# Values of the residue grouping with queries on partitions, in a hybrid DeltaNet and dilated-attention layer

## The chip, the cores and the metric

The kernel runs on one core of one Trainium2 chip. The metric is the time of the device for one execution, in microseconds (us); the time of a kernel is the median of its runs.

## The reference

One decoder layer on a sequence of 2048 positions with a model width of 1024. One input projection feeds two groups of heads; their outputs are concatenated, multiplied by `w_out`, gated, added to `x` and normalised. What matters here is the attention group: 8 heads of width 64, three patterns of causal attention whose results are merged by the softmax of their log-sum-exps.

```
PATTERNS = ((128, 1), (512, 4), (2048, 16))
for window, dilation in PATTERNS:
    o, lse = strided_window_attention(q, k, v, dilation, window // dilation)
    outs.append(o); lses.append(lse)
wts = jax.nn.softmax(jnp.stack(lses, axis=0), axis=0)
o_at = jnp.sum(wts[..., None] * jnp.stack(outs, axis=0), axis=0)
o_at = rmsnorm(o_at, at_norm_w) * jax.nn.silu(at_z)
mix = jnp.concatenate([o_dn, o_at], axis=-1) @ w_out
```

Each position sees, per pattern, itself and earlier positions at steps of the dilation, up to the window.

## The kernel before, in words

The kernel has three stages, one after the other. The first (projections, the chunked delta rule) isn't touched. The second is the attention, and the third what is left of the output projection.

**The attention.** The heads are worked on in 4 pairs `p`, and the sequence in 4 blocks `blk` of 512 positions. Within a block there are 8 units of work. Four belong to grouping *a* (the pattern of dilation 1): 128 queries against at most 256 neighbouring keys. Four belong to grouping *b*, the grouping by residues `r` of the position modulo 4: 128 queries of one residue against all keys of that residue so far, `(blk + 1) * 128` of them, with one mask that serves both the pattern of dilation 4 and that of dilation 16. So for each pair there are 4 units of *b* with one tile of 128 keys, 4 with two, 4 with three and 4 with four.

A unit has three steps. `scores` (L1211) multiplies queries and keys into PSUM (tile `s`), adds the mask and takes the extremum on VectorE (`sm`), and exponentiates on ScalarE (`p`, queries on partitions). `turn` (L1236) transposes `p` on TensorE, 128x128 at a time, two tiles of keys and both heads to a PSUM bank `tr` (two banks), and copies each bank to SBUF (`pts`, keys on partitions), three in four copies on VectorE and the fourth on ScalarE. `values` (L1255) multiplies by the values: for each tile of keys `k` and each head `hd` of the pair, a matmul whose stationary operand (`lhsT`) is the head's 64 columns of `v`, and whose moving operand (`rhs`) is the head's 128 columns of `pts`. The output stands with the 64 value columns on partitions: head 0 on partitions 0 to 63, head 1 on 64 to 127, of one PSUM bank `po` (a single buffer), 128 queries per unit side by side. In the fourth unit of a grouping ScalarE copies the bank to SBUF, as `oa` (L1369) or `ob` (L1384).

All data is fp32. Queries and keys are split into fp32r halves; `p`, `pts` and `v` are plain fp32, and a plain fp32 matmul of the program is two weight loads and two MATMUL instructions in the trace. A transposition is one of each.

**The merge.** `combine` (L1263) runs once per pair and block, 16 times, as a generator in the queue `aux`. It sends the statistics of grouping *a* through DRAM (`sscr`) to bring them to the order of *b*, waits some units of work, forms the two weights `ca` and `cb` per query and head, and then, for `oa` and for `ob` (L1288 to L1295): takes a bank `tr`, transposes four 128x128 pieces so that queries stand on partitions, multiplies the bank by the weight on VectorE into `cmb`, and yields. The two are added on GpSimd, normalised, transposed back and stored.

**The order of the work.** `attention` (L1389) issues for each unit: its scores; the values of the unit before the last; the transpositions of the last unit. After each of the two yields the driver (L1650) takes one step of the filler queue `side` in every second turn (L1651), which is up to four matmuls of 512 columns of the output projection (`mix_dn` L1552 and `mix_at` L1574; tiles `ip<-w_..,m_..`), and one step of each generator in `aux`. Waits inside generators (`hop`, L213) are counted in TensorE time that the kernel itself adds up for each matmul and transposition (`Counted`, L141). What is left of `mix_at` when the attention has ended runs by itself, through the banks `s`.

Of the kernel before, what the change touches and what calls it, by code (L numbers as in the profile page):

```python
# [21 lines left out]
P = 128  # L22
# [90 lines left out]
def kernel(ctx: ExitStack, tc: tile.TileContext, x, c_t, pos, w_mod, b_mod_t, b_gate,  # L113
# [45 lines left out]
    T, TE, VO, AO = Counted(nc.tensor), Counted(Early(nc.tensor)), InOrder(nc.vector), InOrder(nc.scalar)  # L159
    dma = nc.sync.dma_start  # L160

    def flat(t):
        return t.rearrange("p a b -> p (a b)")
# [6 lines left out]
    def bank(tag, bufs=2):  # L170
        return psum.tile([P, 512], F32, name=tag, tag=tag, bufs=bufs)
# [41 lines left out]
    def hop(n=HOP):  # L213

        end = spent[0] + n * TICK
        yield
        while spent[0] < end:
            yield
# [3 lines left out]
    ident, le, gt, m16, cols = (cst[:, i] for i in range(5))  # L222
# [53 lines left out]
    def rsqrt(pool, y, a, tag):  # L276

        u = pool.tile(list(y.shape), F32, name="rs_u", tag=tag + "_u")
        V.tensor_scalar(y.bitcast(I32), a.bitcast(I32), -0.5, 1597463007.0, op0=OP.mult, op1=OP.add)
        for _ in range(3):  # L280
            V.tensor_tensor(u, y, y, OP.mult)  # L281
            V.scalar_tensor_tensor(u, u, -0.5, a, op0=OP.mult, op1=OP.mult)  # L282
            V.scalar_tensor_tensor(y, u, 1.5, y, op0=OP.add, op1=OP.mult)
# [971 lines left out]
    def values(pts, v, po, q):  # L1255
        for k, p_ in enumerate(pts):
            for hd in range(2):
                T.matmul(po[64 * hd:64 * hd + 64, q * P:q * P + P], lhsT=v(k)[:, 64 * hd:64 * hd + 64],
                         rhs=p_[:, hd], start=k == 0, stop=k == len(pts) - 1)

    combined = [0] * 4

    def combine(pool, p, blk, oa, ob, sta, sb):  # L1263

        gz = pool.tile([P, 4, P], F32, name="agz", bufs=1)
        dma(gz, zscr[p, :, :, blk * P:(blk + 1) * P])
        sa = pool.tile([P, 4, 4], F32, name="stc", bufs=2)
        d = sscr[p, blk]
        dma(d, sta)
        for b in range(4):  # L1270
            dma(sa[32 * b:32 * b + 32], bass.AP(tensor=d.tensor, offset=d.offset + 4 * b,
                                                ap=[[16, 32], [512, 4], [1, 4]]))
        yield from hop(LAG)
        w = pool.tile([P, 4, 4, 2], F32, name="cw_", bufs=2)
        mn, ca, cb, l = (w[:, i] for i in range(4))
        V.tensor_tensor(mn, sa[:, :, 0:2], sb[:, :, 0:2], OP.min)
        V.tensor_tensor(ca, mn, sa[:, :, 0:2], OP.subtract)
        V.tensor_tensor(cb, mn, sb[:, :, 0:2], OP.subtract)
        A.activation(w[:, 1:3], w[:, 1:3], AF.Exp)
        V.tensor_tensor(l, ca, sa[:, :, 2:4], OP.mult)  # L1280
        V.tensor_tensor(mn, cb, sb[:, :, 2:4], OP.mult)
        V.tensor_tensor(l, l, mn, OP.add)
        V.scalar_tensor_tensor(l, l, EPS, l, op0=OP.mult, op1=OP.mult)
        yield
        B4 = [P, 4, 2, 64]
        v4 = "p (t h d) -> p t h d"
        parts = []
        for o_, c_ in ((oa, ca), (ob, cb)):  # L1288
            ps = bank("tr")
            for k in range(4):  # L1290
                T.transpose(ps[:, k * P:k * P + P], o_[:, k * P:k * P + P], ident)
            c = pool.tile(B4, F32, name="cmb", bufs=CMB)
            V.tensor_tensor(c, ps.rearrange(v4, t=4, h=2), c_[:, :, :, None].to_broadcast(B4), OP.mult)
            parts.append(c)
            yield  # L1295
        o, sq = parts
        G.tensor_tensor(o, o, sq, OP.add)
        A.activation(sq, o, AF.Square)
        ssq = pool.tile([P, 4, 2], F32, name="a_ssq", bufs=2)
        V.tensor_reduce(ssq, sq, axis=AX.X, op=OP.add)  # L1300
        V.scalar_tensor_tensor(ssq, ssq, 1.0 / 64, l, op0=OP.mult, op1=OP.add)
        rs = pool.tile([P, 4, 2], F32, name="a_rs", bufs=2)
        rsqrt(pool, rs, ssq, "a")
        G.tensor_tensor(o, o, rs[:, :, :, None].to_broadcast(B4), OP.mult)
        yield from hop(LAG2)
        ps = bank("tr")
        of = o.rearrange("p t h d -> p (t h d)")
        for k in range(4):
            T.transpose(ps[:, k * P:k * P + P], of[:, k * P:k * P + P], ident)
        oc = pool.tile([P, J], F32, name="a_oc", bufs=1)  # L1310
        V.scalar_tensor_tensor(oc, ps, nwz[:, 1:2], flat(gz), op0=OP.mult, op1=OP.mult)
        dma(oscr[1][p, :, :, blk * P:(blk + 1) * P], oc.rearrange("p (r i) -> p r i", r=4))
        combined[blk] += 1
# [3 lines left out]
    def pair_blocks(pool, p):  # L1317

        ks = ahead["k"]
        va, vb = [], []  # L1320
        for blk in range(4):
            (qs, qa), v = ahead["q"], ahead["v"]
            if blk == 1:
                if p < 3:
                    ahead["k"], ahead["load"] = load_k(p + 1)
                else:
                    ya, yb = ahead["y"] = [hp.tile([P, 4, D], F32, name=f"y_{nm}", tag=f"h_{nm}", bufs=2)
                                           for nm in ("hi", "lo")]
                    dma(ya[:, 0], gscr)
                    aux.append(load_w(raws, 4, ya[:, 0], lambda j: yb[:, j // 2, j % 2 * J:j % 2 * J + J], WLAG))  # L1330
            if blk and p < 3:
                ahead["load"](blk - 1, blk)
            elif p and blk == 0:
                ahead["load"](3, 4)
            if blk < 3 or p < 3:
                at = (p, blk + 1) if blk < 3 else (p + 1, 0)
                ahead["q"] = load_q(akp, *at)
                ahead["v"] = load_v(pool, *at)
            va.append(v[0])
            vb.append(v[1])  # L1340
            sta = pool.tile([P, 4, 4], F32, name="sta", bufs=3)
            stb = pool.tile([P, 4, 4], F32, name="stb", bufs=3)
            V.memset(sta, 0.0)
            V.memset(stb, 0.0)
            oa = pool.tile([P, J], F32, name="oa", bufs=2)
            ob = pool.tile([P, J], F32, name="ob", bufs=2)
            box = {}
            for i in range(4):
                b = 4 * blk + i
                n = 256 if b else 128  # L1350

                def part(j, b0, m):
                    return lambda kk: kk[:, j].rearrange("p (r b i) -> p b r i", r=4, b=4)[:, b0:b0 + m]

                if b and not i:
                    rhs = [(slice(0, P), part(blk - 1, 3, 1)), (slice(P, n), part(blk, 0, 1))]
                else:
                    rhs = [(slice(0, n), part(blk, max(i - 1, 0), n // P))]

                def s1(i=i, n=n, rhs=rhs, qa=qa, sta=sta):  # L1360
                    return scores(pool, ks, qa, n, mask_a[:, 256 - n:], sta, i, lambda q: q[:, i], rhs)

                def s3(pts, i=i, b=b, n=n, box=box, oa=oa):
                    if i == 0:
                        box["a"] = bank("po", PO)
                    b0 = b - (n // P - 1)
                    values(pts, lambda k: va[(b0 + k) // 4][:, (b0 + k) % 4], box["a"], i)
                    if i == 3:
                        A.copy(oa.rearrange("p (r b i) -> p r b i", r=4, b=4),  # L1369
                               box["a"].rearrange("p (b r i) -> p r b i", b=4, r=4))  # L1370

                yield s1, lambda pp, n=n: turn(pool, pp, n), s3
            n = (blk + 1) * P
            for r in range(4):
                def s1(r=r, n=n, qs=qs, stb=stb):
                    return scores(pool, ks, qs, n, mask_b[:, J - n:], stb, r, lambda q: q[:, r],
                                  [(slice(0, n), lambda kk: kk[:, 0:n // P, r * P:r * P + P])])

                def s3(pts, r=r, blk=blk, box=box, oa=oa, ob=ob, sta=sta, stb=stb):
                    if r == 0:  # L1380
                        box["b"] = bank("po", PO)
                    values(pts, lambda k: vb[k][:, r], box["b"], r)
                    if r == 3:
                        A.copy(ob, box["b"])  # L1384
                        aux.append(combine(pool, p, blk, oa, ob, sta, stb))

                yield s1, lambda pp, n=n: turn(pool, pp, n), s3
# [362 lines left out]
```

## Time and profile before

| | |
|---|---|
| median of 3 runs | 1560.82 us (1558.38 to 1561.52) |
| the profiled execution | 1564.69 us, its span 1562.9 us |
| TensorE matmuls busy | 1433.8 us (92%) |
| VectorE, ScalarE, GpSimd busy | 1066.2, 656.0, 466.1 us |
| mean granted TensorE clock | 0.975 of 2.4 GHz |

The times stand in microseconds from the start of the span. PE is TensorE's matmul side and PEld its weight loads, which overlap the matmuls; DVE is VectorE, ACT ScalarE, POOL GpSimd, SP the engine that issues the DMAs. A matmul's recorded time contains the latency through the array, so matmuls that follow each other overlap in the record: the spacing of their starts, not the mean time of one, is what one costs. In a timeline, a row of x16 instructions has the start of the first and the time to the end of the last.

### The profile page before, as it was taken

The page shows a single profiled execution, that of the slowest core. Times are in us where ns is not written, and L with a number is a line of the kernel's source. Part 1 is how long each engine was busy: PE and PEld are TensorE (multiplying, and loading weights), DVE is VectorE, ACT ScalarE, POOL GpSimd, SP SyncE. Part 2 cuts the span into 40 slices and gives each one's busy share as a digit, 9 for nine tenths or more (in the row PEclk, how much of TensorE's full clock was granted, in tenths as well). Part 3 has the DMA queues.
Part 4 walks back from the last instruction along what each step waited for, and adds up shares of the span by engine and source line. Part 5 has one row for each costly group of instructions (what it writes and reads, how often), then busy time and mean ns, then how long its engine had stood idle before and what let it go on. Part 6 is the DMA issues. An engine that isn't in the chain of part 4 may idle for free.

```text
span 1562.9 us, 28358 instructions
## 1 busy us (share of the span) xinstructions
PE 1433.8 (92%) x9848; PEld 1156.7 (74%) x9848; DVE 1066.2 (68%) x3305; ACT 656.0 (42%) x1864; POOL 466.1 (30%) x573
## 2 busy tenths in 40 slices
PE   3898999989879999998999999998899998999997
PEld 2687787767767787876777779886677776777776
DVE  6868745684786367587687766434476776889766
ACT  4435234335433753433243343222455554576444
POOL 2424253333452432041231320223121211142243
PEclk9999999999999999999999999999999999999999
DMA  8845562546573642454434515438877637363364
GB/s 245 277 135 192 162 206 81 176 133 212 178 225 97 226 132 87 155 177 129 152 99 129 159 39 154 148 106 259 248 224 212 205 108 229 89 197 104 105 226 162
DMA packets 256336, 257.08 MB, mean 164 GB/s; under 512 B 44993, under 2 KB 196673, under 8 KB 255681
## 3 DMA queue, kind: packets, MB, share of 16 engines
q1 hardware_dynamic: 253744, 246.88, 51.1%
q10 hardware_dynamic: 2448, 8.39, 1.4%
q8 instruction: 78, 1.28, 0.3%
q14 instruction: 66, 0.53, 0.1%
HBM read 164.31 MB, written 90.90 MB: 163 GB/s over the span
## 4 chain that ended last, share of the span: by engine, by line
PE 36%; DVE 10%; DMA 4%; ACT 2%; issue 2%; POOL 1%; SPq 1%; DVEq 0%; ACTq 0%; POOLq 0%
PE ip L149 16%; PE s L149 8%; PE tr L154 5%; PE po L149 4%; PE g L149 2%; PE sc L149 2%; DVE cv_y L693 1%; DMA sscr<-sta 1%; DMA wg<-in_w_mod_dram 1%; DVE tmp_inv L807 1%; DVE rs_u L282 1%; DVE pts L1251 1%; DMA y_lo<-in_w_out_dram 1%; DVE sm L1226 1%; DVE rs_u L281 0%
## 5 line engine op out<-in xcount | busy, mean ns | idle before, releaser
L149 PE MATMUL ip<-h_hi,w_hi 128*128 128x512 f32 x864 | 352.8, 410 | 6.0 <-ACT cv_r L688 4.7
L149 PE MATMUL ip<-h_hi,w_lo 128*128 128x512 f32 x864 | 352.6, 410 | 0.0
L149 PE MATMUL ip<-h_lo,w_hi 128*128 128x512 f32 x864 | 352.5, 410 | 0.0
L149 PEld LDWEIGHTS ip<-h_hi,w_hi 128*128 128x128 f32 x864 | 165.9, 192 | 39.3 <-ACT cv_r L688 5.6
L149 PEld LDWEIGHTS ip<-h_lo,w_hi 128*128 128x128 f32 x864 | 165.3, 191 | 32.2 <-issue 0.5
L149 PEld LDWEIGHTS ip<-h_hi,w_lo 128*128 128x128 f32 x864 | 165.1, 191 | 32.2 <-issue 0.8
L693 DVE SCALAR_TENSOR_TENSOR cv_y<-cv_r,cw,cv_y 128x512 f32<-128x512 f32 x144 | 116.0, 805 | 32.9 <-ACT cv_y L690 23.0
L581 POOL TENSOR_TENSOR w_lo<-w_raw,w_hi 128x512 fp32r<-128x512 f32 x72 | 97.0, 1357 | 112.4 <-ACT w_hi L580 84.7
L1226 DVE CUSTOM_DVE_ANT_0 sm<-s,mask 128x256 f32<-128x256 f32 (+3 forms) x256 | 107.9, 447 | 21.4 <-PE s L149 10.7
L154 PE MATMUL tr<-cst,p 128*128 128x128 f32 x568 | 95.3, 289 | 4.2 <-ACT p L1229 2.7
L1251 DVE COPY pts<-tr 128x512 f32<-128x512 f32 (+1 forms) x120 | 73.1, 616 | 30.7 <-PE tr L154 29.2
L1229 ACT ACTIVATE p<-sm,stb 128x128 f32<-128x128 f32 (+3 forms) x128 | 70.9, 555 | 52.4 <-DVE stb L1226 39.9
L1229 ACT ACTIVATE p<-sm,sta 128x256 f32<-128x256 f32 (+1 forms) x128 | 63.2, 495 | 68.7 <-DVE sta L1226 61.9
L154 PEld LDWEIGHTS tr<-cst,p 128*128 128x128 f32 x568 | 62.1, 142 | 25.4 <-issue 14.6
L695 ACT ACTIVATE cv_t<-cv_y 128x512 f32<-128x512 f32 x48 | 30.3, 631 | 117.6 <-DVE cv_y L693 114.1
L149 PE MATMUL ip<-w_hi,h_hi 128*128 128x264 f32 (+1 forms) x256 | 75.4, 295 | 2.0 <-DVE rp L1033 1.3
L149 PE MATMUL ip<-w_hi,h_lo 128*128 128x264 f32 (+1 forms) x256 | 75.0, 293 | 0.0
L149 PE MATMUL ip<-w_lo,h_hi 128*128 128x264 f32 (+1 forms) x256 | 74.9, 293 | 0.0
L807 DVE TENSOR_TENSOR tmp_inv<-xt_inv,blk 128x8 f32<-128x8 f32 (+14 forms) x240 | 65.6, 273 | 6.4
L580 ACT CAST w_hi<-w_raw 128x512 fp32r<-128x512 f32 x72 | 43.6, 617 | 49.4 <-DMA w_raw<-in_w_in_dram 40.9
L138 ACT ACTIVATE sqo<-o 128x128 f32<-128x128 f32 x64 | 19.8, 309 | 103.0 <-DVE o L138 97.3
L1041 POOL TENSOR_TENSOR rp<-rx,tab 128x512 f32<-128x512 f32 x32 | 41.5, 1312 | 57.5 <-ACT rx L1031 48.5
(470 smaller groups left out, 3372.9 us busy)
## 6 DMA issues: line engine op xcount, KB each, us to landing
w_raw<-in_w_in_dram SPq DMA_DIRECT2D x72, 256.0 KB, 3.9
ws<-w_hi SPq DMA_DIRECT2D x15, 1024.0 KB, 5.5
ws<-w_lo SPq DMA_DIRECT2D x15, 1024.0 KB, 7.4
w_hi<-ws SPq DMA_DIRECT2D x15, 1024.0 KB, 6.0
w_lo<-ws SPq DMA_DIRECT2D x15, 1024.0 KB, 7.5
xt<-in_x_dram SPq DMA_DIRECT2D x24, 512.0 KB, 5.2
wm<-in_w_mod_dram SPq DMA_DIRECT2D x32, 256.0 KB, 5.4
tab<-ctab SPq DMA_DIRECT2D x32, 256.0 KB, 3.3
```

What stands on the lines that cost most here:

```text
L138: return f(*a, **k)
L149: i = self.engine.matmul(ps, lhsT=lhsT, rhs=rhs, **k)
L154: i = self.engine.transpose(*a)
L580: A.copy(hi[:, s, 0:256], raw)
L581: G.tensor_tensor(lo[:, s, 0:256], raw, hi[:, s, 0:256], OP.subtract)
L693: V.scalar_tensor_tensor(y, r[:, n:n + J], cw[:, ti, n:n + 1], y, op0=OP.mult, op1=OP.add)
L695: A.activation(t, y, AF.Tanh)
L807: V.tensor_tensor(tmp[:, :, 0:i + 1], xt[:, :, 0:i + 1], b3[:, i:i + 1, 0:i + 1].to_broadcast([P, 4, i + 1]), OP.mult)
L1041: G.tensor_tensor(p2, xs[1 - ct], tab[1], OP.mult)
L1226: V.tensor_tensor_reduce(out=sm, in0=pp[hd], in1=masks, scale=-0.125, scalar=BIG, op0=OP.add, op1=OP.min, accum_out=st[:, slot, hd:hd + 1])
L1229: A.activation(pt, sm, AF.Exp, scale=-1.0, bias=st[:, slot, hd:hd + 1], accum_out=st[:, slot, 2 + hd:3 + hd])
L1251: V.tensor_copy(pts[:, 0:kn], pt[:, 0:kn])
```

## The change

A second function for the values is added and used in grouping *b* alone: the transposed probabilities become the stationary operand (128 columns) and the head's 64 columns of `v` the moving one, so that the output stands with queries on partitions and the 64 value columns of each head side by side. `combine` then takes `ob` as it is; `oa` is transposed as before. `oa` keeps the old function.

```
+    def values_q(pts, v, po, q):
+        for hd in range(2):
+            c = slice(q * P + 64 * hd, q * P + 64 * hd + 64)
+            for k, p_ in enumerate(pts):
+                T.matmul(po[:, c], lhsT=p_[:, hd], rhs=v(k)[:, 64 * hd:64 * hd + 64],
+                         start=k == 0, stop=k == len(pts) - 1)
@@ combine
         for o_, c_ in ((oa, ca), (ob, cb)):
-            ps = bank("tr")
-            for k in range(4):
-                T.transpose(ps[:, k * P:k * P + P], o_[:, k * P:k * P + P], ident)
+            ps = o_
+            if o_ is oa:
+                ps = bank("tr")
+                for k in range(4):
+                    T.transpose(ps[:, k * P:k * P + P], o_[:, k * P:k * P + P], ident)
             c = pool.tile(B4, F32, name="cmb", bufs=CMB)
             V.tensor_tensor(c, ps.rearrange(v4, t=4, h=2), c_[:, :, :, None].to_broadcast(B4), OP.mult)
@@ pair_blocks, grouping b
-                    values(pts, lambda k: vb[k][:, r], box["b"], r)
+                    values_q(pts, lambda k: vb[k][:, r], box["b"], r)
```

## Rows read from the trace of the kernel before

**Rows 1.** Engines' busy time over the whole span, from the page

```profile
PE 1433.8 (92%) x9848; PEld 1156.7 (74%) x9848; DVE 1066.2 (68%) x3305; ACT 656.0 (42%) x1864; POOL 466.1 (30%) x573
```

**Rows 2.** Busy time in two stretches: the attention, and what follows it

```profile
core 0: us, PE busy (x) PEld busy (x) DVE busy (x) ACT busy (x) POOL busy (x), PEclk, DMA share, GB/s
1114.00:1465.50 351.50, 334.76 (x2712) 264.18 (x2711) 268.14 (x1002) 199.29 (x620) 85.37 (x84) 0.99 0.58 168
1465.50:1563.00 97.50, 84.89 (x374) 69.19 (x371) 64.90 (x170) 40.27 (x91) 37.79 (x30) 0.94 0.52 181
```

**Rows 3.** Groups of instructions: count, busy us, mean ns, idle us before them

```profile
L149 PE MATMUL po<-pts,vb 128*64 128x128 f32 x640 | 50.6, 285 | 4.6 <-ACT pts L1249 2.5 <-ACT oa L1369 1.1 <-DVE pts L1251 0.9
...
L154 PE MATMUL tr<-cst,ob 128*128 128x128 f32 x64 | 10.3, 285 | 4.1 <-DVE cmb L1293 4.0
...
L149 PE MATMUL g<-g,ones 128*128 128x32 f32 x4 | 0.8, 276 | 0.0
```

**Rows 4.** Timeline of PE around a values group with four key tiles

```profile
1454.75 0.39 PE L149 MATMUL ip<-w_lo,m_hi 128*128 128x512 f32 x1
1455.07 1.09 PE L149 MATMUL po<-pts,vb 128*64 128x128 f32 x16
1456.09 1.09 PE L154 MATMUL tr<-cst,p 128*128 128x128 f32 x8
```

**Rows 5.** Timeline of PE around one with a single key tile

```profile
1219.96 0.44 PE L149 MATMUL po<-pts,vb 128*64 128x128 f32 x4
1220.33 0.44 PE L154 MATMUL tr<-cst,p 128*128 128x128 f32 x2
```

**Rows 6.** Timeline of PE, a values group cut after its first, second and third pair

```profile
1301.42 0.33 PE L149 MATMUL po<-pts,va 128*64 128x128 f32 x2
...
1301.42 0.44 PE L149 MATMUL po<-pts,va 128*64 128x128 f32 x4
...
1301.42 0.55 PE L149 MATMUL po<-pts,va 128*64 128x128 f32 x6
```

**Rows 7.** Timeline of PE: filler, transpositions of `ob`, the next values group

```profile
1209.70 0.39 PE L149 MATMUL ip<-w_lo,m_hi 128*128 128x512 f32 x1
1209.93 0.60 PE L154 MATMUL tr<-cst,ob 128*128 128x128 f32 x4
1210.46 0.66 PE L149 MATMUL po<-pts,va 128*64 128x128 f32 x8
1211.05 0.44 PE L154 MATMUL tr<-cst,p 128*128 128x128 f32 x2
```

**Rows 8.** Timeline of PE: plain fp32, 128 stationary and 32 moving columns

```profile
593.49 0.60 PE L149 MATMUL g<-g,cst 128*128 128x32 f32 x4 [0.57 <-DVE sc L751]
593.92 0.39 PE L149 MATMUL g<-g,ones 128*128 128x32 f32 x2
```

**Rows 9.** Waits of the weight loads in the attention: total, times, longest

```profile
PEld tr L154 <- issue: 17.9, 93, 1.4
PEld po L149 <- issue: 14.3, 51, 0.5
PEld tr L154 <- ACT p L1229: 5.9, 21, 1.6
PEld tr L154 <- DVE cmb L1293: 4.5, 2, 4.3
PEld po L149 <- DVE sta L1226: 4.1, 12, 0.4
```

**Rows 10.** Timeline of the longest stop of PE in the attention

```profile
1305.01 0.66 PE L154 MATMUL tr<-cst,p 128*128 128x128 f32 x4
...
1308.96 0.69 DVE L1293 TENSOR_TENSOR cmb<-tr,cw__14528 128x512 f32<-128x512 f32 x1 [5.24 <-DMA sscr<-sta]
...
1309.71 1.12 PE L154 MATMUL tr<-cst,ob 128*128 128x128 f32 x4 [4.04 <-DVE cmb L1293]
```

**Rows 11.** VectorE's products of two tensors, one operand in PSUM, or both in SBUF

```profile
L1045 DVE TENSOR_TENSOR rpc<-rp,rp 128x512 f32<-128x512 f32 x32 | 38.0, 1206 | 11.2 <-POOL rp L1041 11.2
...
L1157 DVE TENSOR_TENSOR mf_x<-ip,mf_x 128x512 f32<-128x512 f32 x8 | 5.5, 690 | 18.7 <-PE ip L149 10.0 <-DMA mf_x<-in_x_dram 6.6 <-issue 2.0
```

## The prediction

> **What bounds the kernel now.** I read the busy times of the whole page first [rows 1]: TensorE's matmuls are busy 92% of the span, VectorE 68%. A share of the whole span says nothing of one stage, so I then asked for the busy times of the two stretches that the change can touch [rows 2]: in the attention (351.5 us) PE is busy 95% and VectorE 76%, and in the 97.5 us behind it PE 87%. Overlapping records make PE look fuller than it is, so the third view is a timeline of PE around one values group [rows 4]: filler, values, transpositions follow each other, and no row names an engine that PE waited for. The waits of the weight loads [rows 9] show the same: the largest by far are "issue" (17.9 and 14.3 us), in which nothing else is late. Waits for other engines sum to some ten microseconds beside them (the softmax 5.9, one bank 4.5; the 12 equal waits of 0.3 to 0.4 us put down to `sta` look like the "issue" ones under another name). So the attention is bound by TensorE's own sequence, and microseconds added to or taken from it there should show nearly one for one. Behind it comes more TensorE work, which only moves.
>
> **How a values group costs what it does.** Grouping *b* has 16 units each with one, two, three and four key tiles (4 pairs x 4 residues). A key tile is two heads with two MATMULs each, so the groups have 4, 8, 12 and 16 instructions: 16 x 40 = 640, the count of [rows 3].
>
> Now: cut after one, two and three pairs, a group reaches 0.33, 0.44 and 0.55 us [rows 6]. The second instruction of a pair adds nothing, each pair adds 0.11. The two heads write different halves of the partitions, and their matmuls run side by side. An instruction thus costs 0.055 us.
>
> At the edges it costs more. From the last filler to the group pass 0.32 us [rows 4], from a filler to transpositions 0.23 [rows 7]: 0.09 more. Four transpositions behind a values group take 0.66 us [rows 10], four behind a filler 0.60 [rows 7]: 0.06 more. The group itself, from its start to the next, takes 1.02 us with 16 instructions [rows 4] and 0.37 with four [rows 5]; 12 instructions between them cost 0.65, and the rest is a fixed part of 0.15. So there is a toll of 0.15 + 0.09 + 0.06 = 0.30 us per group, paid on the way into and out of the half-width form. The whole comes to 0.09 + 0.37 + 0.06 = 0.52 for four instructions, 1.17 for 16 and, on the line between, 0.74 and 0.95. Sum 3.38, times 16: 54.1 us.
>
> The Trainium skill, "TensorEngine Tiling (Array Packing)", section When to Use Tiling, speaks against the change: for a moving width of up to 64 it says to swap the operands so that the narrow one is stationary and two column tiles work at once, and that is the form which is given up here. The trace agrees that this form works (pairs, 0.11 us each); what the page's advice leaves out of its factor of two is the toll, 64 x 0.30 = 19 us here.
>
> **The change, part by part.**
>
> *Values.* The instruction count stays at 640. All 128 columns of the array are now stationary, so nothing runs side by side, and the moving width is 64. The trace has no fp32 matmul of just this shape; the nearest has 128 stationary and 32 moving columns [rows 8]. Four of these need 0.43 us from their start to the next row's (0.108 each); the next two take 0.39, less the 0.276 of one [rows 3], 0.114. I take 0.111: with a quarter of the moving columns of a transposition it is no cheaper, so the weight load sets the pace, and 64 columns still lie under it. The floor would be 0.055 (half of the 0.11 that a pair of 128 columns needs), if the moving columns set the pace; that is the first rival. Going in, the first load lies under the filler or transposition before it, and the last matmul is out after its 64 columns, 0.055 instead of 0.111. There is no toll. So N instructions cost 0.111 N - 0.055: 0.39, 0.83, 1.28, 1.72, sum 4.22, times 16: 67.5 us. Against 54.1 that is **+13.4 us**: -0.13, +0.09, +0.33 and +0.55 per unit with one, two, three and four key tiles. If the first load isn't hidden, 64 x 0.11 = 7.0 more.
>
> *Transpositions of `ob`.* 64 go [rows 3]. Four of them push the next values group 0.53 us back [rows 7], of which 0.09 is that group's toll: 0.44 x 16 = **-7.0 us**, all of it in PE's sequence. What follows is the unit's next step, whose inputs are there; nothing new is late.
>
> *VectorE's product.* It read a PSUM bank and now reads `ob` in SBUF. With one operand in PSUM a product of two tensors takes 0.69 us, with both in SBUF up to 1.21 [rows 11]; so 16 x 0.52 = 8.3 us of VectorE's time at most, and a small gain isn't excluded. VectorE has 83 us free in the attention [rows 2], and the product is awaited by GpSimd alone: nothing. Without that cover, in the densest stretches, it would be a part of the 8.3.
>
> *Waits.* `ob` no longer takes a bank `tr`. The weight load now waits for `pts` and the matmul for `v`, before it was the other way round; both are a unit old by then, and behind them on PE the same transpositions wait. `hop` counts the same for the new matmuls and 0.43 us less per merge for the lost transpositions; the merges come a little earlier, which nothing waits for.
>
> Sum: 13.4 - 7.0 = **+6.4 us**. The rows are of one execution of 1564.69 us, 0.25% above the median of the runs; 1571.1 for that one, and 1560.8 + 6.4 = 1567.2 us for the median.
>
> **The rivals.**
>
> *A: the moving columns set the pace.* 640 x 0.055 = 35.2 us instead of 54.1, with the 7.0: -26 us, **1535 us**. It decides if PE loads the next weights faster than 0.055 us. The matmuls with 32 moving columns [rows 8] speak against it, as they would then be under 0.03 apart; for it speaks only that those are few, of another stage. The Trainium skill, "TensorE: Matmul & The Clock Gate", section Back-to-back issue gap, gives moving columns over the clock as the gap of a matmul by itself, which is this rival; its section LDWEIGHTS gives columns over 1.2 GHz, 107 ns for 128, whatever moves, which is the forecast. The trace's 0.108 to 0.114 sides with the second.
>
> *B: waits give it back.* The longest stop of PE [rows 10] ends in the transpositions of `ob`: VectorE waited 5.24 us for a store of statistics, the two banks `tr` were full, and PE stood 4.0 us. Without these transpositions scores and filler could have gone on. The transpositions behind the stop took 1.12 us instead of 0.60 [rows 7, 10], so PE was at its lower clock (1.2 instead of 2.4 GHz); a few such microseconds cost one or two more. If all of the 4.3 us and of that go, 6.0 are back: +0.4, **1561 us**. Against it: the store is just as late, and PE stops at the next transposition of `p`, which needs a bank as well.
>
> *C: the costs at their upper ends.* First loads not hidden (+7.0), and the units with one key tile, where PE does wait at times, give back nothing of their 16 x 0.13 = 2.1: 6.4 + 9.1 = +15.5, **1576 us**. Against it: weight loads overlap the matmuls before them elsewhere in the trace.
>
> **How the numbers follow.** The forecast, with its own range of 1563 to 1571, gets 0.58; A 0.08, B 0.20, C 0.14. Two measured times of this kernel can be told apart from about 0.2%, 3.1 us. Slower than 1563.9: nearly all of the forecast (0.54) and C, 0.68. Within: B's middle and the low end of the forecast, 0.20. Faster: A and the outer part of B, 0.12. The range leaves out A and the upper part of C: 1559 to 1574.
>
> **What would show it.** In the trace after: `po<-pts,vb` stays at 640, its starts some 0.11 us apart, one by one and not in pairs; a group with 16 instructions takes 1.7 us to the next row and one with four 0.4 to 0.45; transpositions behind it take 0.60 for four; "issue" waits of the weight loads fall to about half, those around *a* stay; `tr<-cst,ob` is gone; the attention is some 6 us longer, and what follows it as long as before. Starts 0.055 apart would be A. If the starts are 0.11 apart and the time doesn't rise, look at the stops of PE for B.

## The result, and the profile after

The changed kernel took 1579.51 us (median of 4 runs, 1575.51 to 1582.89) against 1561.17 us of the kernel before on the same chip (1558.38 to 1563.65): a ratio of 1.0104 [1.0085, 1.0122], slower by 18.3 us. Measured again with more runs it was 1.0062 [1.0041, 1.0084], slower by 10.6 us. Forecast were +6.4 us and a range up to 1574: the direction was right, the size was not. The profiled execution took 1579.59 us, its span 1577.8.

First the busy times of the whole page, which answer to [rows 1].

```profile
PE 1454.1 (92%) x9784; PEld 1196.9 (76%) x9784; DVE 1069.2 (68%) x3305; ACT 656.4 (42%) x1864; POOL 465.7 (30%) x573
```

64 instructions fewer on PE, 20 us more of its time. Where do they stand? Next the two stretches of [rows 2]: the attention, and what follows it.

```profile
core 0: us, PE busy (x) PEld busy (x) DVE busy (x) ACT busy (x) POOL busy (x), PEclk, DMA share, GB/s
1111.00:1482.00 371.00, 356.06 (x2678) 305.53 (x2679) 275.38 (x1027) 204.63 (x641) 84.63 (x84) 0.97 0.56 164
1482.00:1577.80 95.80, 83.20 (x372) 67.91 (x371) 64.61 (x170) 40.38 (x91) 38.15 (x30) 0.98 0.53 184
```

The attention took 371 us; before it was 351.5 in this cut. From here on I take its length from the first transposition of `p` to the last values group: 356.5 and 354.9 us in two executions of the kernel before, 370.6 and 368.4 in two of the changed one, on average +13.8. What follows took 95.8 us, against 97.5.

Now the new values groups. First the cuts of a group after one, two and three instructions, as in [rows 6], then the group in its surroundings, as in [rows 4].

```profile
1470.00 0.22 PE L149 MATMUL po<-vb,pts 128*128 128x64 f32 x1
...
1470.00 0.33 PE L149 MATMUL po<-vb,pts 128*128 128x64 f32 x2
...
1470.00 0.44 PE L149 MATMUL po<-vb,pts 128*128 128x64 f32 x3
```

```profile
1469.77 0.39 PE L149 MATMUL ip<-w_lo,m_hi 128*128 128x512 f32 x1
1470.00 1.89 PE L149 MATMUL po<-vb,pts 128*128 128x64 f32 x16
1471.73 1.04 PE L154 MATMUL tr<-cst,p 128*128 128x128 f32 x8
...
1474.44 1.89 PE L149 MATMUL po<-vb,pts 128*128 128x64 f32 x16
```

Each instruction adds 0.11 us by itself where a pair did. From filler to group pass 0.23 us (0.32 before), the group takes 1.73 to the next start (1.02 before), and eight transpositions behind it 1.04 (1.09 before): no toll. The groups with 4, 8 and 12 instructions took 0.40, 0.84 and 1.29 (medians of those outside the stretches at the lower clock).

The waits of the weight loads in the attention answer to [rows 9]. "Issue" has fallen from 17.9 and 14.3 us to somewhat less than half; the forecast said about half. The wait for VectorE's copies of `pts` has grown: the last line below is that of the kernel before.

```profile
PEld tr L154 <- issue: 7.9, 43, 0.4
PEld po L149 <- issue: 6.2, 25, 0.4
PEld po L149 <- DVE pts L1251: 6.2, 11, 2.8
PEld tr L154 <- ACT p L1229: 5.6, 18, 0.9
```

```profile
PEld po L149 <- DVE pts L1251: 2.1, 7, 0.5
```

The longest of these waits is a stop of PE, and it answers to [rows 10]. The timeline shows PE and VectorE there.

```profile
1246.59 0.69 DVE L1579 TENSOR_TENSOR m_x<-ip,m_x 128x512 f32<-128x512 f32 x1
...
1248.16 0.60 PE L154 MATMUL tr<-cst,p 128*128 128x128 f32 x4
...
1249.54 0.82 DVE L1284 TENSOR_TENSOR cw__13776<-stc,stb 128x8 f32<-128x8 f32 x1 [2.25 <-DMA stc<-sscr]
...
1250.56 0.68 DVE L1251 COPY pts<-tr 128x512 f32<-128x512 f32 x1
...
1251.30 1.16 PE L149 MATMUL po<-vb,pts 128*128 128x64 f32 x8 [2.54 <-DVE pts L1251]
```

The merge's first product of statistics (L1284) waits 2.25 us on VectorE for the DMA that brings them back from DRAM. VectorE works in its order, so a copy of transposed probabilities stands behind it, and PE stands 2.5 us for that copy. In the kernel before the longest stop lay at another merge and ended in the transpositions of `ob`. The row behind the stop has 1.16 us for eight instructions, where 1.00 is usual: within it, at 1252.2, PE's granted clock falls to 1.2 GHz, and it stays there for a while, as the next section shows.

### The profile page after: what moved, and what is told of

Its sections match the earlier page's. It is cut to its first block, busy times and chain, and to the rows that moved or that the text cites. A ratio compares the mean times of both kernels' runs of the same rounds, so it can differ in the third digit from the quotient of the medians.

```text
span 1577.8 us, 28218 instructions
## 1 busy us (share of the span) xinstructions
PE 1454.1 (92%) x9784; PEld 1196.9 (76%) x9784; DVE 1069.2 (68%) x3305; ACT 656.4 (42%) x1864; POOL 465.7 (30%) x573
## 5 line engine op out<-in xcount | busy, mean ns | idle before, releaser
L149 PEld LDWEIGHTS po<-vb,pts 128*128 128x128 f32 x640 | 81.6, 196 | 13.7 <-ACT pts L1249 3.9
L149 PE MATMUL po<-vb,pts 128*128 128x64 f32 x640 | 84.1, 276 | 7.3 <-DVE pts L1251 2.9
L154 PEld LDWEIGHTS tr<-cst,p 128*128 128x128 f32 x568 | 66.9, 150 | 16.0 <-issue 6.8
```

The lines of the kernel that those rows point to most:

```text
L149: i = self.engine.matmul(ps, lhsT=lhsT, rhs=rhs, **k)
L154: i = self.engine.transpose(*a)
```

## Experiments

All ratios are to the kernel before, measured beside each kernel on the same chip; not all kernels were measured on one chip, so those whose comparisons differ are set side by side by their ratios. Two theories run through the expectations. **ORDER**: the program's text gives dependences and priorities; the framework's scheduler makes the order of each engine from them, and with the transpositions gone it makes another one, in which the merge's work stands ahead of its data. **BANK**: the transpositions held the merge back until a bank `tr` was free, and that pacing was of use. The expectation of a size is what the prediction gave.

**The baseline and the change once more.** No edit.

> The kernel before once more, for a second trace of it. Two theories of why the change cost 18 us and not the 6.4 forecast. SEQUENCE: TensorE's own sequence in the attention grew by more than was worked out (the first pair of traces says some 10 us), and the rest, about 3 us before the attention and 3 in it, is more time at the lower clock, which comes by chance: then the stage before the attention, whose instructions are the same, varies by some 3 us between executions of any of these kernels, and the clock of this one may come out anywhere from 0.970 to 0.976. CLOCK: the changed kernel is held at the lower clock for longer because of what it does: then this one stays near 0.975 and the changed one near 0.970 every time. Time: 1561 either way.

1564.00 us, ratio 0.9990 [0.9972, 1.0009]. The mean granted clock of its profiled execution was 0.971 where it had been 0.975: the mean over the whole span changes by as much between two executions of one kernel.

> The changed kernel once more, for a second trace of it. Both theories: 1579, 1.0% above before. SEQUENCE: in the trace the attention is 10 us longer at the full clock, and the time at the lower clock differs from that of the first trace (24 us in the attention) by as much as it differs between the two traces of before. CLOCK: again 20 us or more at the lower clock in the attention, against 10 to 13 of before, and a mean clock of 0.970.

1575.80 us, 1.0062 [1.0041, 1.0084]. That the kernel before keeps to itself and the change loses about 0.6% is settled. The interval doesn't meet that of the first comparison (1.0085 to 1.0122); why isn't known. In the attention itself the time at the lower clock was 13.3 and 13.7 us in the two executions of the kernel before, and 23.9 and 20.0 us in those of the changed one.

**The values alone**: the change, with `ob` transposed nonetheless (which leaves its values in the wrong place).

```
-            if o_ is oa:
+            if True:
                 ps = bank("tr")
```

> The changed kernel with the transpositions of ob put back (they turn data the wrong way; the output is not the reference's). It isolates what their loss is worth. Forecast's term: 7.0 us, so 1586 against 1579 of the changed kernel. If they were mostly covered, 0 to 3 us (1579 to 1582): then the term of -7.0 was the one that failed.

1577.07 us, 1.0084 [1.0062, 1.0106]: +11.9 us by the medians, +13 by the ratio. The term of +13.4 holds. But the changed kernel, which has 64 transpositions fewer, is only 1.3 us faster than this by the medians (3.4 by the ratios, and the two intervals overlap), not 7.0. The traces show no gain in the attention at all: 370.6 and 368.4 us, against 367.8 with the transpositions kept. Time at the lower clock there is 23.9 and 20.0 us against 15.8, and PE's waits for VectorE's copies of `pts` are 6.2 us in the first of these against 1.5.

**Twice the moving columns**: 128 instead of 64 in `values_q` (both heads' values to the same 128 columns of the output).

```
-            c = slice(q * P + 64 * hd, q * P + 64 * hd + 64)
+            c = slice(q * P, q * P + P)
-                T.matmul(po[:, c], lhsT=p_[:, hd], rhs=v(k)[:, 64 * hd:64 * hd + 64],
+                T.matmul(po[:, c], lhsT=p_[:, hd], rhs=v(k),
```

> The changed kernel with all 128 columns of v as moving operand in each values matmul of grouping b, instead of the head's 64 (both heads write the same columns; the output is not the reference's). If the weight load sets the pace, starts stay 0.109 to 0.112 us apart and only the last of a group costs more: 64 x 0.055 = +3.5 us at most, 1579 to 1583. If the moving columns set it, starts were near 0.055 and become 0.11: +35 us. CLOCK: with twice the columns streamed the clock goes back to 0.975 and some 5 us come back: 1574 to 1578. SEQUENCE: the clock is as in the changed kernel within chance.

1578.18 us, 1.0091 [1.0068, 1.0114]: 2.4 us more than the change, not tens. Within a group the starts stand 0.112 us apart in both kernels (median), and the mean time of one instruction is nearly the same, 280 and 276 ns.

```profile
L149 PE MATMUL po<-vb,pts 128*128 128x128 f32 x640 | 85.9, 280 | 11.6 <-DVE pts L1251 6.7 <-DVE a_rs L279 2.5 <-issue 1.2
```

```profile
L149 PE MATMUL po<-vb,pts 128*128 128x64 f32 x640 | 84.1, 276 | 7.3 <-DVE pts L1251 2.9 <-ACT pts L1249 2.7 <-ACT oa L1379 1.1
```

So the moving columns don't set the pace, and rival A has no ground. What the instructions with 32, 64 and 128 moving columns share is the loading of 128 stationary ones. The trace has 13.7 us at the lower clock in the attention, 6 to 10 less than the change, and yet its attention is longer (372.7 us): the lower clock alone doesn't explain the loss.

**The loss of the transpositions alone**: the kernel before, with `ob` taken as it is (the product then has values in the wrong place).

```
-            ps = bank("tr")
-            for k in range(4):
-                T.transpose(...)
+            ps = o_
+            if o_ is oa:
+                ps = bank("tr")
+                for k in range(4):
+                    T.transpose(...)
```

> The kernel before without the transpositions of ob (its values are as before, so the product of combine reads ob the wrong way round; the output is not the reference's). The mirror of ob_kept. Forecast's term: -7.0 us against before. PARTLY COVERED (ob_kept cost 1.3 us in time, and some 4 in its trace at the full clock): -1 to -4 us.

1568.56 us, 1.0028 [1.0004, 1.0052]: the kernel with less work is *slower* by 4 us, where the sum has -7.0. The interval only just leaves out 0, but it leaves out -7.0 by far. This is the step that failed. PE's order is another one: of the 2676 matmul instructions that the trace has in the attention, at least 196 stand out of the order of the kernel before (compared by tile and shape), though only 16 groups of four transpositions were taken out. The two executions of the kernel before don't differ in a single place. PE's waits for VectorE's copies of `pts` rose from 2.1 us to 13.8, the longest 3.9:

```profile
PEld po L149 <- DVE pts L1251: 13.8, 15, 3.9
```

That longest one is a stop at the same merge as the changed kernel's:

```profile
1241.93 0.60 PE L154 MATMUL tr<-cst,p 128*128 128x128 f32 x4
...
1243.70 1.11 DVE L1276 TENSOR_TENSOR cw__13776<-stc,stb 128x8 f32<-128x8 f32 x1 [3.31 <-DMA stc<-sscr]
...
1246.22 0.66 PE L149 MATMUL po<-pts,vb 128*64 128x128 f32 x8 [3.69 <-DVE pts L1251]
```

Behind such stops stand stretches at the lower clock. Three views follow, of the kernel before, of the changed one and of this one: windows laid on the stretches of the attention whose granted clock (the third number from the end) is 0.50, that is 1.2 GHz.

```profile
1309.60:1313.00 3.40, 3.29 (x12) 2.76 (x12) 1.84 (x7) 0.88 (x4) 1.28 (x1) 0.51 0.55 154
1398.30:1405.10 6.80, 6.09 (x31) 5.02 (x31) 5.52 (x19) 4.66 (x14) 4.38 (x4) 0.50 0.73 245
```

```profile
1252.20:1255.60 3.40, 3.40 (x14) 2.88 (x13) 1.45 (x9) 2.07 (x8) 0.00 (x0) 0.50 0.36 108
1320.50:1330.70 10.20, 9.73 (x39) 8.99 (x40) 5.99 (x33) 3.68 (x15) 3.47 (x4) 0.50 0.83 255
1412.60:1419.40 6.80, 5.81 (x28) 5.81 (x29) 5.08 (x20) 3.67 (x13) 3.81 (x4) 0.50 0.63 231
```

```profile
1247.50:1250.90 3.40, 3.40 (x17) 2.42 (x15) 2.04 (x10) 1.70 (x7) 0.00 (x0) 0.50 0.46 133
1312.30:1319.10 6.80, 5.84 (x24) 4.07 (x25) 6.05 (x31) 3.56 (x14) 2.77 (x3) 0.50 0.78 244
1401.10:1411.30 10.20, 8.42 (x43) 6.83 (x43) 8.72 (x32) 6.43 (x22) 5.44 (x6) 0.50 0.47 155
```

10 us of them before, 20 after, 20 with the transpositions merely gone (a stretch of up to 3.4 us at the very start of the attention, in all three, is left out here and counted in the totals elsewhere). The first of each begins at the end of the longest stop or within 1.5 us of it; the others begin in or up to 1.8 us behind stops of 1.0 to 1.9 us. Not every such stop has one: 1.50 us at 1214.8 in the kernel before, and 1.42 at 1393.6 in this one, have none. A microsecond at half the clock loses up to half of itself, so 10 us more of them are some 5 us.

**The change in the first block only**, where groups have four instructions and are cheaper in the new form.

```
+                    (values_q if blk == 0 else values)(pts, ..., box["b"], r)
+            if o_ is oa or not (blk == 0):
```

> The new form of the values, and ob taken as it is, only in the first block of each pair, where a unit has one key tile; the other blocks as before. By the forecast's law for a group (0.111 N - 0.055 us against a toll of 0.30 and 0.055 N): 16 x -0.13 = -2.1 us for the values, and 4 of the 16 merges without transpositions, -1.0 (partly covered) to -1.8: -3 to -4 us against before. If short groups gain nothing because PE waits beside them: 0 to -1.

1563.01 us, 0.9997 [0.9976, 1.0018]: no change by the medians, where 3 to 4 us were expected; the interval reaches down to -3.7 us. It points the same way as the last one: what is taken out of PE's work doesn't come back as time.

**Fewer tolls**: the kernel before, with the values of two units issued one behind the other, PE in program order in the attention.

```
-VD = 1
+VD = 2
-                    f, pts = w2.popleft()
-                    f(pts)
+                    while w2:
+                        f, pts = w2.popleft()
+                        f(pts)
+            ordered[0] = 1      (ahead of the attention's loop; 0 behind it)
+PT = 6, CMB = 3                 (buffers of pts and cmb; 5 and 4 before)
```

> The kernel before with the values of two units issued together, in the order of the program in the attention (65 values groups instead of 125), six buffers pts instead of five and three cmb instead of four; values in the old half-width form, transpositions of ob as before. If the toll of 0.30 us per group is real: 60 x 0.30 = -18 us, less what VectorE and ScalarE now come late with, since values wait a unit longer: -10 to -18 against before. If the toll is a wait that only shows itself there, and PE would have waited anyway: 0.

1593.38 us, 1.0183 [1.0152, 1.0213]: far off. The attention took 385.8 us, 47.6 of it at the lower clock. Most of this is the fixed order, which costs 1.0155 by itself (*ordered* below); against that, too, some 60 tolls fewer brought nothing. The same with the scheduler's order and five buffers:

> The kernel before with the values of two units issued one after the other, the order left to the scheduler (93 values groups instead of 125), buffers as before. The toll alone: 32 x 0.30 = -9.6 us in PE's sequence. pairs6o, with 65 groups in a fixed order, lost 29 us, and the run ordered showed that a fixed order alone loses 28. So -3 to -10 against before, unless the longer way from scores to values makes new stops.

1562.99 us, 1.0010 [0.9987, 1.0034]. Even. The trace has 93 values groups, and a joined one is cheaper: 1.90 us for 32 instructions, where two groups of 16 take 1.02 each. Other waits take the place of the gain: for products of the filler's input (`m_x`) 5.0 us where there were 1.8, for VectorE's copies of `pts` 4.7 where there were 2.1; and 19.7 us of the attention are at the lower clock.

**A later merge.** The constant that holds the merge back behind the sending of its statistics (L1273), in the changed kernel, in the kernel before, and in the kernel without the transpositions:

```
-LAG = 4.0
+LAG = 6.5
```

> The changed kernel with the merge's first VectorE work later (LAG 6.5 instead of 4.0). In both traces of the changed kernel PE stops for 2.8 to 3.1 us where VectorE stands at that work before its statistics have landed, and the clock is lower right behind it. STOPS: without that stop 3 us and 1.5 to 3 us of lower clock come back: 1570 to 1573 against 1576, and the lower clock falls from 20 us or more in the attention to some 13. CHANCE: nothing moves.

1568.39 us, 1.0023 [1.0001, 1.0045], against 1.0062 of the change as it is. By the middle values nearly two thirds of the loss are gone; the two intervals just meet. But the stop didn't vanish, as was expected of it; it lies at nearly the same point of the attention, at another merge's statistics, and ends in transpositions:

```profile
1237.78 0.17 DVE L1284 TENSOR_TENSOR cw__13807<-stc,stb 128x8 f32<-128x8 f32 x1 [2.47 <-DMA stc<-sscr]
...
1242.06 1.39 PE L154 MATMUL tr<-cst,p 128*128 128x128 f32 x4 [2.48 <-ACT p L1229]
```

Between the two VectorE works through what the wait held up, and the work on the scores that `p` needs (`sm`) stands behind it. The attention took 362.2 us, 13.7 of it at the lower clock, as in the kernel before.

> The kernel before with LAG 6.5 instead of 4.0, as in lag6. ORDER (the place of the merge among the units moves stops and time at the lower clock, in any of these kernels): the time moves by some us either way. If it gains 5 us or more here too, lag6 says nothing of the change; if 0 to +3, the later merge suits the changed kernel alone.

1563.14 us, 0.9996 [0.9977, 1.0015]: the later merge gives the kernel before nothing, so it isn't simply a better setting. (In the one trace its attention is shorter, 351.2 us with 3.4 at the lower clock, and what follows longer, 100.7.)

> The kernel before with LAG 6.5 and without the transpositions of ob (the output is not the reference's). ORDER: with the merge at a place that does no harm the loss is worth 4 to 7 us against before_lag6, and the lower clock takes no more time in the attention than there. If it is slower again, the loss itself does the harm, wherever the merge stands.

1559.10 us, 0.9976 [0.9957, 0.9996], 4.0 us under the kernel before with the same delay (3.1 by the ratios; the intervals overlap). With the later merge the loss of the transpositions is a gain at last, at the lower edge of what was expected or just under it, and 8 us better than the same loss with the merge where it was (0.9976 against 1.0028, intervals apart). The trace doesn't bear out the second half of the expectation, that the stretches at the lower clock go: it has 20.0 us of them in the attention, against 3.4 of the kernel before with that delay. Nor is the attention shorter in it, 352.2 us against 351.2; where the 4 us come from, one trace of each doesn't show.

**PE in program order.** If ORDER holds, the sum must come out where the order can't change: the kernel before, the same without the transpositions, and the whole change, each with

```
+            ordered[0] = 1
             for i, _ in enumerate(attention(ap_)):
...
             over.append(1)
+            ordered[0] = 0
```

> The kernel before with TensorE's instructions of the attention issued strictly in the order of the program, instead of in the order that the scheduler of the framework makes of it. It is the base for the next two, in which that order then stays the same but for the change. By itself: PE waits where it was let past before, 0 to +10 us against before.

1590.81 us, 1.0155 [1.0119, 1.0191]: 28 us slower, where 0 to 10 were expected. PE stops for 9.4 us soon after the attention begins, and 58 us of the attention are at the lower clock, against 13.

> The kernel before in the order of the program, without the transpositions of ob (the output is not the reference's). Without a fixed order their loss made the kernel before 4 us slower (no_ob). ORDER: what cost the 7 us of the forecast, and more, was the other order that the scheduler made, with stops at other places and more time at the lower clock: with the order fixed the loss gives 4 to 7 us against the run ordered. COVERED: the transpositions stood where PE waited anyway: 0 to 2 us.

1584.68 us, 1.0133 [1.0105, 1.0162]: -6.1 us by the medians, -3.4 by the ratios, against a forecast of -7.0. Here PE's order in the attention differs from that of the kernel above by the missing transpositions and nothing else; so does that of the next. The intervals overlap widely, so the gain isn't clear of noise.

> The changed kernel with TensorE in the order of the program in the attention. ORDER: against the run ordered it shows the forecast's own sum, +6.4 us (4 to 9). COVERED: +12 to +14, the values' 13.4 with little given back.

1597.92 us, 1.0210 [1.0178, 1.0242]: +7.1 us over *ordered* by the medians, +8.6 by the ratios, against a forecast of +6.4. The three are slow kernels and their intervals are wide: signs and sizes are those of the sum, but the sizes are known to some 6 us only. The attention of the three, from the traces:

```profile
1103.30:1495.60 392.30, 354.68 (x2747) 276.82 (x2747) 277.10 (x1025) 204.54 (x639) 84.72 (x84) 0.93 0.52 155
```

```profile
1108.70:1492.20 383.50, 342.75 (x2687) 265.74 (x2687) 274.71 (x1025) 204.83 (x639) 84.28 (x84) 0.94 0.54 159
```

```profile
1101.50:1494.20 392.70, 360.54 (x2687) 308.61 (x2688) 277.72 (x1025) 205.33 (x639) 84.49 (x84) 0.95 0.52 154
```

In these traces the whole change costs the attention 0.4 us, not 7. The executions are an uneven pair: that of *ordered* took 1595.47 us, among its slowest, that of *ordered_after* 1593.04, its fastest; the time at the lower clock is 58 us in the first, 44 in the second and 40 in the third.

**BANK**: the changed kernel, in which the merge takes a bank `tr` for `ob` with one transposition instead of four (the product reads that one piece four times).

```
-            ps = o_
-            if o_ is oa:
-                ps = bank("tr")
-                for k in range(4):
-                    T.transpose(...)
+            ps = bank("tr")
+            for k in range(4 if o_ is oa else 1):
+                T.transpose(...)
```

> The changed kernel with one of the four transpositions of ob put back, so that the merge takes a bank tr for ob again and PE does a quarter of that work (the product uses that one piece four times; the output is not the reference's). BANK: if taking a bank there keeps the merge's place, it has the order of ob_kept and three quarters of the gain, 5 us: 1572 where ob_kept was 1577 and the changed kernel 1576. TIME: nothing to gain, 1576 to 1577.

1577.92 us, 1.0080 [1.0052, 1.0108]. No better than the change: taking the bank alone brings nothing back, and BANK finds no support. It isn't refuted, for PE's order here isn't that of *ob_kept* either (at least 115 of 2691 instructions stand out of it).

**The statistics' buffers**: more of them in the kernel before, so that the next unit's statistics needn't wait.

```
-            sta = pool.tile([P, 4, 4], F32, name="sta", bufs=3)
+            sta = pool.tile([P, 4, 4], F32, name="sta", bufs=5)     (stb too)
```

> The kernel before with five buffers for each statistics tile (sta, stb) instead of three. The longest stop of PE in both its traces (4.0 to 4.3 us) ends when VectorE, which stood at clearing a statistics tile until its last store had landed, goes on; the clock is lower for 3.4 us behind it. The order of PE stays nearly the same. STOPS: the stop goes, and with it the lower clock behind it: -4 to -6 us against before. If another wait takes its place: 0.

1563.97 us, 1.0009 [0.9985, 1.0032]. The longest stop shrank from 4.04 to 2.38 us, the stretch of 3.4 us at the lower clock behind it stayed, and so did the time: a stop isn't a price that can be taken off by itself.

**Two attempts at something better than both**: the new form in the first two blocks with the later merge, and the two units' values together with it.

> The new form of the values, and ob taken as it is, in the first two blocks of each pair (one and two key tiles to a unit), the rest as before, with LAG 6.5. By the law for a group 16 x (-0.13 + 0.09) = -0.6 us for the values, and 8 of the 16 merges without transpositions, -1.5 (by no_ob_lag6 against before_lag6) to -3.5: -2 to -4 us against before, 1558 to 1560. If short groups gain nothing: 0.

1565.63 us, 1.0022 [1.0004, 1.0040]: slower, where 2 to 4 us of gain were expected.

> The kernel before with the values of two units issued one after the other (order left to the scheduler) and LAG 6.5. pairs5 had some 6 us less in PE's sequence than before and 6 us more in stops, and came out even. If the later merge makes fewer stops here, as in the changed kernel: -3 to -8 against before. If the stops come from the longer way between scores and values: 0.

1563.44 us, 1.0000 [0.9984, 1.0017]. Both missed. No version that computes the layer beat the kernel before.

## Why the prediction was right, and where it was wrong

*What bounds the attention*: right for time that is added. It is TensorE's sequence, and the values' extra time came through nearly one for one. For time taken away the "nearly one for one" didn't hold, as the transpositions show.

*The values, +13.4 us*: right. The groups take 0.40, 0.84, 1.29 and 1.73 us against 0.39, 0.83, 1.28 and 1.72; the toll is gone on both sides; the change with the transpositions kept costs 12 to 13 us. The 0.30 us per group is what the half-width form paid at its edges, and it vanished with it; that fewer tolls alone come back as time isn't shown (*pairs5*, *pairs6o*). The Trainium skill, "TensorEngine Tiling (Array Packing)", section Key Properties, says that a change of tiling mode drains the engine. The trace agrees with it as far as time at these edges goes (from a filler to a group 0.32 us before, 0.23 after).

*VectorE's product from SBUF, nothing*: right. Of the 16 products of `ob` in the trace after, 14 took 0.68 us, as those from PSUM do, and two took 1.10 and 1.28: 1.0 us in all, of the 8.3 that were the bound. GpSimd alone waits for them.

```profile
1261.89 0.68 DVE L1303 TENSOR_TENSOR cmb<-tr,cw__13776 128x512 f32<-128x512 f32 x1
1262.48 0.68 DVE L1303 TENSOR_TENSOR cmb<-ob,cw__13776 128x512 f32<-128x512 f32 x1
```

*The transpositions, -7.0 us, "all of it in PE's sequence ... nothing new is late"*: **this failed**, and with it the size. Their loss was worth 1.3 us by the medians (3.4 by the ratios) in the changed kernel, and in the kernel before it cost 4 us. I had read the order of the trace as if it were fixed, and taken 16 pieces out of it. It isn't fixed: the scheduler made another one, with differences all through the attention, in which VectorE meets the merge's statistics before they have landed. Two sentences of the prediction on waits are the same mistake: that the merges "come a little earlier, which nothing waits for", and that the values' operands "are a unit old by then". VectorE waits for the statistics, the copies of `pts` come late behind that, and PE waits for the copies: 6.2 us in the changed kernel and 13.8 in *no_ob*, against 2.1 before. The time at the lower clock, which the sum put at nothing without a reason, grew from 13 to between 20 and 24 us.

That the worth of the loss hangs on where the merge stands is shown: with the merge where it was the ratio is 1.0028 [1.0004, 1.0052], with the merge put off 0.9976 [0.9957, 0.9996], and putting it off does nothing for the kernel before. That the sum of +6.4 was that of a kernel whose order stays is argued, not shown. Where the order was held, the loss brought 3 to 6 us (not clear of noise) and the whole change cost 7 to 9, to within some 6 us; where the merge was put off, the loss brought 3 to 4, and the whole change cost 4 (*lag6* against *before_lag6*, by the ratios 0.0027 of 1563 us), both with intervals that overlap.

Where the 13.8 us of the attention lie I split by the spacing of PE's starts (the usual spacing of each pair of neighbours at full clock, what goes beyond it, and what the lower clock adds). In the two executions of each kernel the usual spacing sums to 322.3 and 322.4 us before and 332.8 and 332.0 after; waits to 23.2 and 24.5, and 23.5 and 22.0; the excess at the lower clock to 10.9 and 8.1, and 14.3 and 14.4. So PE's sequence grew by 10 us, the clock's share by 5, and the waits in all by nothing: those that went (the longest stop at `ob`, many of the "issue" ones) make up for those that came. With the transpositions kept the sequence is 337.1: the values add 14.8 to it, and the loss takes back 5 of the 7. By this estimate the term of -7.0 was mis-sized by 2 us, that of the values by 1, and 5 us of lower clock were missing from the sum. The clock's share is its firmest part. The line between sequence and waits isn't: with medians over all kernels as the usual spacing, kept apart by the place in a group, the sequence grew by 17 us and the waits shrank by 8, while the clock's share grew by 5 again.

*Rival A* fell with the starts at 0.11 us and with *wide_move*. *Rival B* had the right place and the wrong sign: the stop at `ob` went, but others came, and the lower clock took more time instead of less. *Rival C*'s time was near the measured one for another reason: the first loads are hidden, as the 0.23 us from filler to group shows. Its smaller part, that the short groups give nothing back, fits *q_blk0*.

**What stays open.** Which part of the loss is the order, and which the clock, isn't separated: *no_ob_lag6* was faster than its counterpart while its trace had more time at the lower clock, and *sta5* with a shorter stop gained nothing. *wide_move*, too, had less time at the lower clock than the change, and was no faster. A kernel with the scheduler's old order written out for the changed one wasn't tried; it would be the direct test. Nor is it known why the same change measured 1.0104 and 1.0062. One source of such differences can be seen: the stage ahead of the attention is the same work in all kernels, and yet took from 1101.5 to 1113.5 us (from 1102.6 without the three in program order). Here it is in a second execution of the kernel before and in *wide_move*:

```profile
0.00:1113.50 1113.50, 1016.50 (x6739) 824.61 (x6740) 729.11 (x2111) 412.55 (x1135) 343.50 (x459) 0.97 0.51 160
```

```profile
0.00:1102.60 1102.60, 1010.83 (x6739) 821.12 (x6740) 731.57 (x2111) 412.67 (x1135) 343.52 (x459) 0.98 0.51 162
```

The same 6739 matmuls, 10.9 us apart, with 68.3 and 54.6 us at the lower clock. Differences of 5 us between totals of single executions say nothing here, and many runs are needed. Lengths of one stage say more, but not much more: the attention differed by 1.6 and 2.2 us between two executions of one kernel, and in the traces of *ordered_after* and *no_ob_lag6* it doesn't show what the many runs do.

## What to carry to other kernels

Here a narrow matmul whose two column halves work side by side cost half as much per instruction (0.055 us against 0.11), but a fixed toll for each excursion into that form (0.30 us). By the times of the groups short runs of it (four instructions) lose and long runs (sixteen) win by a third; the kernel that gave up the form in the short runs alone was no faster for it. Work taken off the bounding engine was no sure gain here, where the order didn't stay: where a scheduler makes the order, a removed instruction can move much of what stands behind it, so forecast such a gain with a lower bound below zero, and test it once with the order held. Here VectorE met a wait of 2 to 3 us for a DMA, and the copy queued behind it stopped PE for 2.5 to 3.7 us; after a change of order look first at such waits.

## What the runs showed of the hardware

- A plain fp32 matmul instruction with 128 stationary columns cost 0.11 us with 32, 64 and 128 moving columns alike (0.108 to 0.114). Before the runs only the first and last of these stood in the trace, the last as transpositions.
- In the traces of the kernel before, the change and *no_ob*, stretches at 1.2 GHz of 3.4, 6.8 or 10.2 us began in, or up to 1.8 us behind, stops of PE of 1.0 to 4.0 us; some were many times the stop's own length. Other stops of 1.0 to 1.6 us had none. In *ordered* such stretches sum to 58 us of an attention of 392.
- VectorE's product of two tensors of 128x512 took 0.68 us with an operand in PSUM, and the same with both in SBUF in 14 of 16 cases.
- The longest stop lies at the same place in each execution of one kernel (4.0 us at 1310 and 3.8 us at 1314 in the kernel before, whose attentions began 5 us apart): it belongs to the program's order, not to chance.
